# One layer of a diffusion backbone on one core: expert chunks of eight adjacent tiles, their inputs loaded a chunk ahead, and gate tables built in lagged steps

## The chip, the cores and the metric

The kernel runs on one core of one Trainium2 chip. The metric is device time in microseconds (us) from one execution; the engines are PE (matrix products, with weight loads shown as PEld), DVE (vector), ACT (scalar and activations), POOL and SP. SP, ACT and POOL also issue DMAs, each in its own program order, on queues that share 16 DMA engines.

## The reference, cut to what matters

The layer mixes tokens (attention and pooling, not touched here) and then runs a product-key expert sub-layer over 512 tokens. Each token has 8 heads with 16 experts each, out of 16,384; every expert is one row of `peer_u` and one row of `peer_v`:

```python
gate = jax.nn.softmax(top_s, axis=-1).astype(h.dtype)
u = peer_u[eidx]
act = jax.nn.gelu(jnp.einsum('thkd,td->thk', u, hb), approximate=False)
v = peer_v[eidx]
return jnp.einsum('thk,thkd->td', gate * act, v)
```

## The kernel before

The expert sub-layer takes two routes. For 160 of the tokens (called slots: 128 tokens, and 32 more packed four ways) POOL gathers the rows of `peer_u` and `peer_v` by indirect DMA, 1 MB each, and DVE multiplies them (L706) or accumulates them into `acc0` (L718). There are 320 such slots; `pump` deals them out between other work, each costing DVE one instruction over 2048 columns.

For the other 352 tokens (`TD`) the layer is computed densely. The 16,384 experts are 128 tiles of 128. A **U tile** (`u_tile`, L755) is 48 matmuls that give the activations of one tile for 352 tokens; ScalarE applies GELU (L757). The activations are multiplied by a dense table of gates (DVE, L959), split into a high and a low part (`split`: ACT L120 writes `a_hi`, DVE L121 writes `a_lo`), and a **V pass** (L976) multiplies them with `peer_v`. All products are made of three matmuls of high and low parts, so every weight block of 512 KB is loaded by SP into a `raw` buffer (L136), copied to `whi` by ACT (L120) and subtracted to `wlo` by DVE (L121). There are three `whi`/`wlo` pairs and, in the V stage, five raw buffers (three `raw`, one of `ub`, one `raw_v`).

Two stages matter. In the **spill stage** 72 U tiles are computed ahead, their activations written to `sg_s`, and between them `combine` builds the gate table: for four tokens at a time DVE compares index columns with a ramp (L, L804, one instruction for four tokens; R, L810, one per token, which also multiplies by the gate), PE forms `pg` from L and R (L811), ACT copies `pg` into `ge` (L812), and after 44 tokens `ge` (one buffer) goes to `g_s` by one DMA of 2,816 KB issued by ACT.

In the **V stage** the 128 tiles are taken in 16 chunks of eight (`CH`). A chunk is four fresh U tiles, then four tiles from `sg_s` (loaded by SP, L958, into three `sg` buffers that fresh tiles use too), then four passes `dq` over quarters of the output, each of 96 matmuls over the chunk's eight tiles; the last two chunks hold only kept tiles. The fresh tiles come first in a pass, the kept ones last. Sums go to `acc` by DVE (L987). After chunk 14 the gathered tokens are finished, after chunk 15 the dense ones.

A scheduler sets each engine's order from the program text; engines run their own list in order, so an instruction that waits holds everything behind it on its engine, the DMAs it issues included.

## Time and profile before

| | |
|---|---|
| runs (three) | 3627.98, 3633.67, 3633.84 us; median 3633.67 |
| profiled execution | 3620.55 us, of which the span from first to last instruction is 3618.8 |
| spill stage in the span | 1342 to 2048 us |
| V stage in the span | 2048 to 3602 us |
| mean granted PE clock | 0.977 of 2.4 GHz |

The span is one execution; a stage's length comes from the start of its first and last matmuls. A PE matmul of 352 columns is shown about 0.32 us long but the next one starts 0.16 us after it, since they overlap; so PE's pace is read from starts, or from counts in a stretch, and its losses from the idle time before an instruction and from the clock. A row of instructions reads: start, length, engine, line, operation, output and inputs; in square brackets stand the idle time before it and what ended it.

### The profile page before, as it was taken

To read this page: it belongs to the slowest core of one execution; us is meant where nothing else is said; L and a number is where in the kernel's file an instruction comes from. 1 tells how busy PE (TensorE), PEld (TensorE's weight loads), DVE (VectorE), ACT (ScalarE), POOL (GpSimd) and SP (SyncE) were. 2 spreads that over 40 slices of the span, in tenths; PEclk is the share of its full clock that TensorE was granted. 3 is DMA by queue.
4 is the path that set the end of the run, shared out by engine and by line. 5 is a ranking of instruction groups with operands and counts; after the bars stand their busy time and mean duration, and the time that the engine had idled before them with its cause. 6 is when DMAs were issued, how large, how long until landed. Compare 5 with 4: busy or idle time off the path is not lost.

```text
span 3618.8 us, 52598 instructions
## 1 busy us (share of the span) xinstructions
PE 3415.4 (94%) x20467; PEld 3159.7 (87%) x20467; DVE 2746.1 (76%) x4078; ACT 1383.3 (38%) x1981; POOL 562.5 (16%) x455
## 2 busy tenths in 40 slices
PE   7899999999998999999998999999999999999998
PEld 2588888899887889999988999899999998999998
DVE  5787787756536999997878677777777777877785
ACT  7455545455323234444443322233333222333343
POOL 1000000000031001211222222222212211222210
PEclk9999999999999999999999999999999999999999
DMA  9755555422547227889888879888878888888884
GB/s 338 266 174 171 177 169 179 149 66 75 197 140 252 83 91 260 299 321 345 322 312 309 323 289 336 305 305 296 312 296 315 304 308 313 323 309 307 313 309 166
DMA packets 267205, 916.01 MB, mean 253 GB/s; under 512 B 27666, under 2 KB 83707, under 8 KB 223179
## 3 DMA queue, kind: packets, MB, share of 16 engines
q1 hardware_dynamic: 157290, 469.45, 37.5%
q0 software_dynamic: 50208, 350.28, 25.5%
q10 hardware_dynamic: 59456, 92.92, 7.7%
q8 instruction: 160, 2.62, 0.3%
q14 instruction: 91, 0.74, 0.1%
HBM read 851.27 MB, written 49.71 MB: 249 GB/s over the span
## 4 chain that ended last, share of the span: by engine, by line
PE 57%; issue 15%; DMA 10%; DVE 10%; POOL 4%; ACT 3%; ACTq 0%; SPq 0%; POOLq 0%; DVEq 0%
PE pv L976 15%; PE pu L755 10%; PE pv L755 6%; PE zl L285 6%; PE pq L637 4%; PE zc L285 4%; PE pw L557 4%; DMA aw<-in_ada_dram 3%; DMA sg<-sg_s 2%; POOL row L700 2%; DMA g_s<-ge 2%; DVE wlo L121 2%; PE sc L373 2%; PE pg L811 1%; PE o L404 1%
## 5 line engine op out<-in xcount | busy, mean ns | idle before, releaser
L120 ACT CAST whi<-raw 128x1024 fp32r<-128x1024 f32 x591 | 619.2, 1050 | 1279.7 <-PE pv L976 467.9
L121 DVE TENSOR_TENSOR wlo<-raw,whi 128x1024 fp32r<-128x1024 f32 x591 | 732.3, 1245 | 333.7 <-ACT whi L120 331.9
L976 PE MATMUL pv<-a_hi,whi 128*128 128x352 f32 x2048 | 672.7, 331 | 35.9 <-ACT a_hi L120 30.2
L976 PE MATMUL pv<-a_lo,whi 128*128 128x352 f32 x2048 | 674.7, 330 | 31.3 <-DVE a_lo L121 31.2
L976 PE MATMUL pv<-a_hi,wlo 128*128 128x352 f32 x2048 | 668.6, 329 | 14.4 <-DVE wlo L121 14.3
L976 PEld LDWEIGHTS pv<-a_hi,whi 128*128 128x128 f32 x2048 | 392.9, 193 | 43.9 <-ACT a_hi L120 35.6
L976 PEld LDWEIGHTS pv<-a_lo,whi 128*128 128x128 f32 x2048 | 396.3, 194 | 38.3 <-DVE a_lo L121 38.3
L976 PEld LDWEIGHTS pv<-a_hi,wlo 128*128 128x128 f32 x2048 | 394.7, 193 | 19.6 <-DVE wlo L121 19.4
L755 PE MATMUL pu<-f_hi,whi 128*128 128x352 f32 x1152 | 380.7, 330 | 4.1 <-ACT whi L120 3.4
L755 PE MATMUL pu<-f_hi,wlo 128*128 128x352 f32 x1152 | 377.6, 328 | 6.9 <-DVE wlo L121 6.9
L755 PE MATMUL pu<-f_lo,whi 128*128 128x352 f32 x1152 | 375.8, 326 | 0.0
L718 DVE SCALAR_TENSOR_TENSOR acc<-row,w,acc 128x2048 f32<-128x2048 f32 x127 | 297.9, 2346 | 4.5 <-DMA row<-in_v_dram,eB 4.5
L755 PE MATMUL pv<-f_hi,wlo 128*128 128x352 f32 x896 | 290.4, 324 | 0.0
L755 PE MATMUL pv<-f_lo,whi 128*128 128x352 f32 x896 | 290.2, 324 | 0.0
L755 PE MATMUL pv<-f_hi,whi 128*128 128x352 f32 x896 | 289.1, 323 | 0.0
L706 DVE SCALAR_TENSOR_TENSOR row<-row,f 128x2048 f32<-128x2048 f32 x121 | 275.6, 2284 | 3.3 <-DMA row<-in_u_dram,e 3.3
L285 PE MATMUL zl<-h_hi,whi 128*128 128x512 f32 (+1 forms) x640 | 239.3, 374 | 0.0
L755 PEld LDWEIGHTS pu<-f_hi,wlo 128*128 128x128 f32 x1152 | 220.1, 191 | 9.4 <-DVE wlo L121 9.3
L755 PEld LDWEIGHTS pu<-f_hi,whi 128*128 128x128 f32 x1152 | 220.7, 192 | 6.0 <-ACT whi L120 5.0
L285 PE MATMUL zl<-h_lo,whi 128*128 128x512 f32 (+1 forms) x640 | 223.9, 350 | 0.0
L285 PE MATMUL zl<-h_hi,wlo 128*128 128x512 f32 (+1 forms) x640 | 223.8, 350 | 0.0
L755 PEld LDWEIGHTS pu<-f_lo,whi 128*128 128x128 f32 x1152 | 220.4, 191 | 0.0
(277 smaller groups left out, 6569.7 us busy)
## 6 DMA issues: line engine op xcount, KB each, us to landing
raw<-in_ut_dram SPq DMA_DIRECT2D x234, 512.0 KB
raw<-in_vd_dram SPq DMA_DIRECT2D x205, 512.0 KB
aw<-in_ada_dram SPq DMA_DIRECT2D x256, 256.0 KB
raw<-in_win_dram SPq DMA_DIRECT2D x80, 512.0 KB
aw<-in_ada_dram SPq DMA_DIRECT2D x64, 512.0 KB
raw_v<-in_vd_dram SPq DMA_DIRECT2D x51, 512.0 KB
g_s<-ge ACTq DMA_DIRECT2D x8, 2816.0 KB
gt<-g_s ACTq DMA_DIRECT2D x32, 704.0 KB
```

The costliest lines, as they stand in the source:

```text
L120: S.copy(dst_hi, src)
L121: V.tensor_sub(dst_lo, src, dst_hi.bitcast(F32))
L285: E.matmul(part[0], x[:, k8, :], y[:, k, part[1]], start=k == 0 and p == 0, stop=k == KT - 1 and p == 2)
L373: E.matmul(sc[:, cs], x[:, m, qs], y[:, cs], start=p == 0, stop=p == 1)
L404: E.matmul(po[:, b, :], aT[:, kb, b * 128:(b + 1) * 128], d["vn"][:, kb, :], start=kb == 0, stop=kb == 5)
L557: E.matmul(pw[b], x[:, k, bs], y[:, j, :], start=i + j == 0 and p == 0, stop=i + j == KT - 1 and p == 2)
L637: E.matmul(pq[:, cs], a[:, k8, :], b[:, k, cs], start=k == 0 and p == 0, stop=k == KT - 1 and p == 2)
L700: G.indirect_dma_start(out=row, out_offset=None, in_=table, in_offset=bass.IndirectOffsetOnAxis(ap=e[:, j:j + 1], axis=0))
L706: tc.keep_in_program_order(V.scalar_tensor_tensor(row, row, 1.0, f0, op0=OP.mult, op1=OP.mult, accum_out=s0[:, j:j + 1]))
L718: tc.keep_in_program_order(V.scalar_tensor_tensor(acc0, row, w0[:, j:j + 1], acc0, op0=OP.mult, op1=OP.add))
L755: E.matmul(pu, a[:, k8, :], b[:, k, :], start=k == 0 and p == 0, stop=k == KT - 1 and p == 2)
L976: E.matmul(pv[i], x[:, j, ks], y, start=n + j == 0 and p == 0, stop=n + j == CH - 1 and p == 2)
```

## The change

1. **Chunks.** A chunk is now eight adjacent tiles. `KEPT` says how many of each chunk are kept ones (6, 4, 4, 4, repeated): 72 in all as before, but spread over all 16 chunks, and they come first in the chunk. The fresh tiles (two or four) come last.
2. **Loads.** The gates of a chunk come by one DMA (one buffer `gt` for eight tiles), the kept activations in pairs into `sk` buffers of their own. ACT issues them, in the chunk before: the gates in pass 0, the pairs in passes 1 to 3. SP issues no activations any more.
3. **Gating** of kept tiles is done in pairs (128x704), between the U tiles; that of a fresh tile is put behind the next weight block (`owing`).
4. **`raw_v` is gone**: four raw buffers in the V stage, as in the spill stage.
5. **Combining.** R becomes one comparison of four tokens on DVE (L828), and ACT scales it by the gate, four instructions (L831). The products follow one step later and the copy to `ge` two steps after that, with four `pg` buffers for two. `ge` stays one buffer.
6. **The end.** The gathered slots finish in chunk 15, and so does `first_end` (the code that stood after chunk 14). `g2c` is made in the spill stage; `few_end_steps` (not shown) uses the `eq` buffers.

```diff
-SPILL = 72
 CH = 8
+KEPT = (6, 4, 4, 4) * 4
+SPILL = sum(KEPT)
...
-RATE = (SLOTS - (SPILL - PRE - GS) * GRATE) / (2 * NKEY - SPILL - 11)
+RATE = (SLOTS - (SPILL - PRE - GS) * GRATE) / (2 * NKEY - SPILL - 8)
+LAG = 2
...
-            sg = ub.tile([128, NG, TG], F32, name="sg", bufs=3)
+            return pu
+        def activated(pu):
+            sg = ub.tile([128, NG, TG], F32, name="sg", bufs=2)
             S.activation(sg.rearrange("p a t -> p (a t)"), pu, AF.Gelu)
             return sg
         def spill(n):
             for _ in range(n):
-                ib = next(run_ahead)
-                sg = u_tile(ib, psU.tile([128, TD], F32, name="pu", bufs=2))
-                nc.scalar.dma_start(sg_s[ib], sg.rearrange("p a t -> p (a t)"))
-        run_ahead = iter(range(SPILL))
+                i, ib = next(run_ahead)
+                sg = activated(u_tile(ib, psU.tile([128, TD], F32, name="pu", bufs=2)))
+                nc.scalar.dma_start(sg_s[i], sg.rearrange("p a t -> p (a t)"))
+        run_ahead = iter(list(enumerate(CH * c + i for c, k in enumerate(KEPT) for i in range(k))))
...
             def combine():
+                ready, made = [], []
+                def products():
+                    g, t4, L, R = ready.pop(0)
+                    pg = ps.tile([128, 4, 128], F32, name="pg", bufs=LAG + 2)
+                    for i in range(4):
+                        E.matmul(pg[:, i, :], L[:, i, :], R[:, i, :], start=True, stop=True)
+                    made.append((g, t4, pg))
+                def copied():
+                    g, t4, pg = made.pop(0)
+                    if t4 == 0:
+                        ges[g] = gb.tile([128, 128, TG], F32, name="ge", bufs=1)
+                    S.copy(ges[g][:, :, t4:t4 + 4].rearrange("p b t -> p t b"), pg)
+                    if t4 + 4 == TG:
+                        nc.scalar.dma_start(g_s[g], ges[g])
+                ges = {}
                 for g in range(NG):
-                    ge = gb.tile([128, 128, TG], F32, name="ge", bufs=1)
                     for t4 in range(0, TG, 4):
-                        m = min(4, TG - t4)
-                        pg = ps.tile([128, 4, 128], F32, name="pg", bufs=2)
-                        L = gb.tile([128, 4, 128], F32, name="L", bufs=2)
                         b, t = divmod(T - TD + g * TG + t4, 128)
-                        V.tensor_tensor(L, iota[:, None, :].to_broadcast([128, 4, 128]),
-                                        picks[b][:, 0, t:t + 4, None].to_broadcast([128, 4, 128]), op=OP.is_equal)
-                        for i in range(m):
-                            b, t = divmod(T - TD + g * TG + t4 + i, 128)
-                            pT = picks[b]
-                            R = gb.tile([128, 128], F32, name="R", bufs=6)
-                            V.tensor_scalar(R, iota, pT[:, 1, t:t + 1], pT[:, 2, t:t + 1], op0=OP.is_equal, op1=OP.mult)
-                            E.matmul(pg[:, i, :], L[:, i, :], R, start=True, stop=True)
-                        S.copy(ge[:, :, t4:t4 + m].rearrange("p b t -> p t b"), pg[:, 0:m, :])
-                        if t4 + 4 < TG:
-                            yield
-                    nc.scalar.dma_start(g_s[g], ge)
+                        pT = picks[b]
+                        L, R = (gb.tile([128, 4, 128], F32, name=n, bufs=3) for n in ("L", "R"))
+                        for x, i in ((L, 0), (R, 1)):
+                            V.tensor_tensor(x, iota[:, None, :].to_broadcast([128, 4, 128]),
+                                            pT[:, i, t:t + 4, None].to_broadcast([128, 4, 128]), op=OP.is_equal)
+                        for i in range(4):
+                            S.activation(R[:, i, :], R[:, i, :], AF.Copy, scale=pT[:, 2, t + i:t + i + 1])
+                        if ready:
+                            products()
+                        if len(made) > LAG:
+                            copied()
+                        ready.append((g, t4, L, R))
+                        yield
+                while ready or made:
+                    if ready:
+                        products()
+                    copied()
                     yield
...
-            nsteps = NG * ((TG + 3) // 4)
+            nsteps = NG * (TG // 4) + LAG + 1
...
-        more.append(lambda shape: fn.tile(shape, F32, name="raw_v"))
...
-            fresh, kept = list(range(SPILL, NKEY)), list(range(SPILL))
-            order = []
-            while fresh:
-                order += fresh[:4] + kept[:4]
-                fresh, kept = fresh[4:], kept[4:]
-            order += kept
             NC = NKEY // CH
+            first = [sum(KEPT[:c]) for c in range(NC)]
+            gts, sks = {}, {}
+            def load_gates(c):
+                if c < NC:
+                    gts[c] = ab.tile([128, NG, CH * TG], F32, name="gt", bufs=1)
+                    tc.keep_in_program_order(nc.scalar.dma_start(gts[c], g_s[:, :, c * CH:(c + 1) * CH, :].rearrange("a p b t -> p a (b t)")))
+            def load_kept(c, ps_):
+                for p in ps_ if c < NC else ():
+                    if 2 * p < KEPT[c]:
+                        sks[c, p] = ab.tile([128, 2, TD], F32, name="sk", bufs=max(KEPT) // 2)
+                        i = first[c] + 2 * p
+                        tc.keep_in_program_order(nc.scalar.dma_start(sks[c, p], sg_s[i:i + 2].rearrange("b p t -> p b t")))
+            def gated(c, n, m, sg, A):
+                V.tensor_tensor(sg.rearrange("p b (a t) -> p b a t", a=NG), sg.rearrange("p b (a t) -> p b a t", a=NG),
+                                gts[c][:, :, n * TG:(n + m) * TG].rearrange("p a (b t) -> p b a t", b=m), op=OP.mult)
+                hi, lo = A[n // 2]
+                split(hi[:, n % 2:n % 2 + m, :], lo[:, n % 2:n % 2 + m, :], sg)
+            def first_end():
...
+            load_gates(0)
+            load_kept(0, range(4))
             for c in range(NC):
-                ibs = order[c * CH:(c + 1) * CH]
+                ibs = list(range(c * CH, (c + 1) * CH))
                 last = c == NC - 1
-                A = []
-                for n, ib in enumerate(ibs):
-                    if n % 4 == 0:
-                        gt = ab.tile([128, NG, 4 * TG], F32, name="gt", bufs=2)
-                        nc.scalar.dma_start(gt, g_s[:, :, ib:ib + 4, :].rearrange("a p b t -> p a (b t)"))
-                    if ib >= SPILL:
-                        sg = u_tile(ib, bank()[:, 0:TD])
-                    else:
-                        sg = ub.tile([128, NG, TG], F32, name="sg", bufs=3)
-                        nc.sync.dma_start(sg.rearrange("p a t -> p (a t)"), sg_s[ib])
-                    V.tensor_mul(sg, sg, gt[:, :, (n % 4) * TG:(n % 4 + 1) * TG])
-                    a_hi = ab.tile([128, TD], F32R, name="a_hi", bufs=CH + 1)
-                    a_lo = ab.tile([128, TD], F32R, name="a_lo", bufs=CH + 1)
-                    split(a_hi, a_lo, sg.rearrange("p a t -> p (a t)"))
-                    A.append((a_hi, a_lo))
-                    if ib >= SPILL:
-                        pump(RATE)
+                A = [tuple(ab.tile([128, 2, TD], F32R, name=n, bufs=CH // 2) for n in ("a_hi", "a_lo")) for _ in range(CH // 2)]
+                owing = []
+                for j in range(CH - KEPT[c]):
+                    n = KEPT[c] + j
+                    pu = u_tile(ibs[n], bank()[:, 0:TD])
+                    pump(RATE)
+                    while owing:
+                        owing.pop(0)()
+                    for p in range(j, KEPT[c] // 2, CH - KEPT[c]):
+                        gated(c, 2 * p, 2, sks[c, p], A)
+                    owing.append(lambda n=n, pu=pu: gated(c, n, 1, activated(pu).rearrange("p a t -> p (a t)")[:, None, :], A))
+                while last and done[0] < SLOTS:
+                    pump(1)
                 for dq in range(4):
                     pp = [banks()[:, :, 0:TD] for _ in range(2)]
                     pv = [pp[i // 2][:, i % 2, :] for i in range(4)]
                     for n in range(0, CH, 2):
                         hi, lo = weights(vd[ibs[n] // 2, dq], [128, 2, 512])
                         for j in range(2):
-                            a_hi, a_lo = A[n + j]
+                            a_hi, a_lo = (x[:, j, :] for x in A[n // 2])
                             for i in range(4):
                                 ks = slice(i * 128, (i + 1) * 128)
                                 for p, (x, y) in enumerate(((hi, a_hi), (hi, a_lo), (lo, a_hi))):
                                     E.matmul(pv[i], x[:, j, ks], y, start=n + j == 0 and p == 0, stop=n + j == CH - 1 and p == 2)
-                        pump(0.5 * RATE)
+                        if not last:
+                            pump(0.5 * RATE)
+                        while owing:
+                            owing.pop(0)()
+                        if n == 4:
+                            if dq == 0:
+                                load_gates(c + 1)
+                            else:
+                                load_kept(c + 1, (dq - 1,))
                         if last and n == 2 and dq:
                             turned(dq - 1, fg)
                     if last:
+                        if dq == 0:
+                            first_end()
                         fg = final_g(dq)
...
-                if c == NC - 2:
-                    while done[0] < SLOTS:
-                        pump(1)
-                    for dq in range(4):
```

What moves is shown at three places. The first is SP's list in one V chunk. Before (`sg` are the kept activations, all else weight blocks):

```order
L136 DMA raw_v<-in_vd_dram 128x1024
L136 DMA raw<-in_vd_dram 128x1024 x3
L136 DMA raw_24646<-in_vd_dram 128x1024
L958 DMA sg<-sg_s 128x352 x2
L136 DMA raw_v<-in_vd_dram 128x1024
L136 DMA raw<-in_vd_dram 128x1024
L958 DMA sg<-sg_s 128x352 x2
L136 DMA raw<-in_vd_dram 128x1024 x2
L136 DMA raw_24806<-in_vd_dram 128x1024
```

and in the changed kernel:

```order
L138 DMA raw<-in_vd_dram 128x1024 x2
L138 DMA raw_23963<-in_vd_dram 128x1024
L138 DMA raw<-in_vd_dram 128x1024 x3
L138 DMA raw_24095<-in_vd_dram 128x1024
L138 DMA raw<-in_vd_dram 128x1024 x3
```

The activations have left SP's list, and with them `raw_v`. They stand on ACT's list now, in the passes of the chunk before (`gt` the gates, `sk` a pair of kept tiles, `sg` a fresh one):

```order
L122 CAST whi<-raw_20852 128x1024
L763 ACTIVATE sg<-pv 128x352
L122 CAST a_hi<-sg 128x352
L968 DMA gt<-g_s 128x8x352
L122 CAST whi<-raw 128x1024 x3
L122 CAST whi<-raw_20984 128x1024
L975 DMA sk<-sg_s 128x2x352
L122 CAST whi<-raw 128x1024 x3
L122 CAST whi<-raw_21116 128x1024
L975 DMA sk<-sg_s 128x2x352
L122 CAST whi<-raw 128x1024 x3
L122 CAST whi<-raw_21246 128x1024
```

The second place is DVE's list in one V chunk. Before, at the turn from the last fresh tiles to pass 0 (`row` and `acc` are gather slots):

```order
L959 TENSOR_TENSOR sg<-sg,gt 128x352 x3
L121 TENSOR_TENSOR wlo<-raw_v,whi 128x1024
L121 TENSOR_TENSOR a_lo<-sg,a_hi 128x352
L706 SCALAR_TENSOR_TENSOR row_12694,s_13314<-row_12694,f_9445 128x2048
L121 TENSOR_TENSOR a_lo<-sg,a_hi 128x352 x2
L121 TENSOR_TENSOR wlo<-raw,whi 128x1024
L959 TENSOR_TENSOR sg<-sg,gt 128x352
L706 SCALAR_TENSOR_TENSOR row_12693,s_13314<-row_12693,f_9445 128x2048
L121 TENSOR_TENSOR a_lo<-sg,a_hi 128x352
L959 TENSOR_TENSOR sg<-sg,gt 128x352
L121 TENSOR_TENSOR wlo<-raw,whi 128x1024
L121 TENSOR_TENSOR a_lo<-sg,a_hi 128x352
```

and in the changed kernel, in passes 1 and 2 of the chunk before:

```order
L979 TENSOR_TENSOR sk<-sk,gt 128x704
L123 TENSOR_TENSOR wlo<-raw,whi 128x1024
L709 SCALAR_TENSOR_TENSOR row_12694,s_13305<-row_12694,f_9445 128x2048
L1045 TENSOR_TENSOR accT<-accT,pv 128x704 x2
L123 TENSOR_TENSOR wlo<-raw_21926,whi 128x1024
L709 SCALAR_TENSOR_TENSOR row_12695,s_13305<-row_12695,f_9445 128x2048
L123 TENSOR_TENSOR wlo<-raw,whi 128x1024
L979 TENSOR_TENSOR sk<-sk,gt 128x704
L123 TENSOR_TENSOR wlo<-raw,whi 128x1024
L709 SCALAR_TENSOR_TENSOR acc_12692,s_13305<-acc_12692,f_9445 128x2048
L123 TENSOR_TENSOR wlo<-raw,whi 128x1024
L1045 TENSOR_TENSOR accT<-accT,pv 128x704 x2
```

Four multiplications of kept tiles stood within pass 0 ahead of weight blocks; now each pair is multiplied one chunk earlier. The third place is one stretch of combining. DVE before:

```order
L804 TENSOR_TENSOR L<-iota,pT 128x512
L810 TENSOR_SCALAR R<-iota,pT 128x128 x4
L121 TENSOR_TENSOR wlo<-raw,whi 128x1024
L804 TENSOR_TENSOR L<-iota,pT 128x512
L810 TENSOR_SCALAR R<-iota,pT 128x128 x2
L121 TENSOR_TENSOR wlo<-raw,whi 128x1024
L718 SCALAR_TENSOR_TENSOR acc_12691<-row_12693,w_13313,acc_12691 128x2048
L810 TENSOR_SCALAR R<-iota,pT 128x128 x2
L804 TENSOR_TENSOR L<-iota,pT 128x512
```

The same on DVE in the changed kernel:

```order
L123 TENSOR_TENSOR wlo<-raw,whi 128x1024
L828 TENSOR_TENSOR R<-iota,pT 128x512
L123 TENSOR_TENSOR wlo<-raw,whi 128x1024
L828 TENSOR_TENSOR L<-iota,pT 128x512
L828 TENSOR_TENSOR R<-iota,pT 128x512
L123 TENSOR_TENSOR wlo<-raw,whi 128x1024
L721 SCALAR_TENSOR_TENSOR acc_12692<-row_12694,w_13304,acc_12692 128x2048
L123 TENSOR_TENSOR wlo<-raw_15959,whi 128x1024
L828 TENSOR_TENSOR L<-iota,pT 128x512
L828 TENSOR_TENSOR R<-iota,pT 128x512
```

Four R instructions have become one. Their multiplication by the gate stands on ACT (four L831 for one step, between the copies of weights):

```order
L831 ACTIVATE R<-R,pT 128x128 x4
L122 CAST whi<-raw 128x1024
L763 ACTIVATE sg<-pu 128x352
L817 COPY ge<-pg 128x4x128
L770 DMA sg_s<-sg 128x352
L831 ACTIVATE R<-R,pT 128x128 x4
L122 CAST whi<-raw 128x1024
L122 CAST whi<-raw_15225 128x1024
```

The copies to `ge` follow a tile's GELU there, and each belongs to a step made earlier.

## Rows read from the trace of the kernel before

**Rows 1.** The page's first lines: busy time of each engine over the whole span.
```profile
span 3618.8 us, 52598 instructions
PE 3415.4 (94%) x20467; PEld 3159.7 (87%) x20467; DVE 2746.1 (76%) x4078; ACT 1383.3 (38%) x1981; POOL 562.5 (16%) x455
```

**Rows 2.** Busy time by stretch, for the spill stage and the V stage: length, busy time and count of PE, PEld, DVE, ACT, POOL, then granted PE clock, DMA engines' busy share, GB/s.
```profile
1342.00:2048.00 706.00, 661.03 (x4189) 649.05 (x4187) 603.28 (x918) 284.38 (x332) 144.20 (x99) 0.97 0.84 308
2048.00:3602.00 1554.00, 1472.44 (x8867) 1451.66 (x8868) 1183.04 (x1114) 480.08 (x593) 316.04 (x223) 0.97 0.82 302
```

**Rows 3.** What PE's matmuls waited for in the V stage: us in total, times, longest.
```profile
PE pv L976 <- DVE a_lo L121: 31.2, 20, 4.2
PE pv L976 <- ACT a_hi L120: 30.2, 16, 5.9
PE pv L976 <- DVE wlo L121: 14.3, 10, 3.1
PE pv L976 <- ACT whi L120: 5.6, 9, 1.0
```

**Rows 4.** Busy time by stretch, columns as in rows 2: chunks 1, 13 and 15.
```profile
2153.30:2255.40 102.10, 95.72 (x578) 94.55 (x577) 77.59 (x81) 30.40 (x36) 22.71 (x16) 0.97 0.84 308
...
3373.70:3471.20 97.50, 94.02 (x578) 92.20 (x577) 80.83 (x73) 32.66 (x41) 24.52 (x16) 1.00 0.89 334
...
3536.40:3602.10 65.70, 65.70 (x421) 65.18 (x420) 40.01 (x55) 24.55 (x40) 0.00 (x0) 1.00 0.43 141
```

**Rows 5.** The same columns: the four U tiles of chunk 1, then the four V passes of chunks 1, 10 and 13.
```profile
2153.40:2184.10 30.70, 30.70 (x193) 30.70 (x193) 22.09 (x24) 10.96 (x14) 7.04 (x4) 1.00 0.63 236
...
2184.10:2255.40 71.30, 64.92 (x386) 63.75 (x385) 55.41 (x57) 19.44 (x22) 15.67 (x13) 0.95 0.93 340
...
3104.60:3172.70 68.10, 64.33 (x385) 63.14 (x385) 56.03 (x45) 19.47 (x22) 14.39 (x13) 0.97 0.96 357
3404.50:3471.20 66.70, 63.22 (x385) 61.40 (x385) 58.49 (x53) 21.70 (x27) 17.31 (x13) 1.00 1.00 379
```

**Rows 6.** DVE in order of time, in pass 0 of chunk 4.
```profile
2507.24 0.53 DVE L959 TENSOR_TENSOR sg<-sg,gt 128x352 f32<-128x352 f32 x1 [3.39 <-DMA sg<-sg_s]
2507.68 1.39 DVE L121 TENSOR_TENSOR a_lo<-sg,a_hi 128x352 fp32r<-128x352 f32 x3
...
2513.52 0.52 DVE L959 TENSOR_TENSOR sg<-sg,gt 128x352 f32<-128x352 f32 x1 [2.25 <-DMA sg<-sg_s]
```

**Rows 7.** SP's DMA issues at the same place (the length of a row of two reaches from the first issue to the end of the second).
```profile
2498.18 0.33 SPq L136 DMA_DIRECT2D raw<-in_vd_dram  x1
2498.61 9.94 SPq L958 DMA_DIRECT2D sg<-sg_s  x2
2515.21 0.33 SPq L136 DMA_DIRECT2D raw<-in_vd_dram  x1
```

**Rows 8.** PE in order of time, at the same place.
```profile
2508.25 0.66 PE L976 MATMUL pv<-a_lo,whi 128*128 128x352 f32 x1 [3.52 <-DVE a_lo L121]
...
2509.30 0.49 PE L976 MATMUL pv<-a_lo,whi 128*128 128x352 f32 x1
2509.59 0.49 PE L976 MATMUL pv<-a_hi,wlo 128*128 128x352 f32 x1
...
2511.91 0.32 PE L976 MATMUL pv<-a_hi,whi 128*128 128x352 f32 x1
2512.07 0.32 PE L976 MATMUL pv<-a_lo,whi 128*128 128x352 f32 x1
```

**Rows 9.** What PE's matmuls waited for in the spill stage, columns as in rows 3.
```profile
PE pg L811 <- ACT ge L812: 13.4, 5, 7.2
PE pg L811 <- DVE R L810: 11.4, 7, 4.3
PE pu L755 <- DVE wlo L121: 6.9, 8, 3.8
PE pt L835 <- DVE zB L836: 4.6, 1, 4.6
PE pv L921 <- ACT sg L757: 4.5, 1, 4.5
PE pu L755 <- ACT whi L120: 3.4, 2, 2.7
```

**Rows 10.** Groups of instructions in the spill stage, DVE's and then ACT's: count, busy time and mean ns of one, idle time before them and what ended it.
```profile
L810 DVE TENSOR_SCALAR R<-iota,pT 128x128 f32<-128x128 f32 x352 | 103.6, 346 | 18.0 <-PE pg L811 17.9
...
L804 DVE TENSOR_TENSOR L<-iota,pT 128x512 f32<-128x512 f32 x88 | 59.8, 679 | 0.0
...
L120 ACT CAST whi<-raw 128x1024 fp32r<-128x1024 f32 x145 | 151.0, 1049 | 286.9 <-PE pu L755 242.5 <-DMA g_s<-ge 8.4 <-issue 6.7
L812 ACT COPY ge<-pg 128x512 f32<-128x512 f32 x88 | 97.2, 1145 | 75.0 <-DMA g_s<-ge 53.3 <-PE pg L811 13.0 <-PE pu L755 8.6
...
L682 ACT ACTIVATE gt<-gt 128x128 f32<-128x128 f32 x3 | 0.9, 309 | 5.8 <-DVE gt L681 5.8
```

**Rows 11.** ACT in order of time at the turn from the spill stage to the V stage.
```profile
2029.31 0.33 ACTq L815 DMA_DIRECT2D g_s<-ge  x1
...
2044.83 0.38 ACTq L953 DMA_DIRECT2D gt<-g_s  x1
2045.30 1.04 ACT L120 CAST whi<-raw 128x1024 fp32r<-128x1024 f32 x1 [8.36 <-DMA g_s<-ge]
```

More of the change, by code (lines that the diff above doesn't have):

```diff
@@ L658, in body @@
         gateB = gp.tile([128, GB], F32, name="gateB")
+        g2c = gp.tile([128, KT], F32, name="g2c")
         eB = gp.tile([128, GB], I32, name="eB")
@@ L823, in few_end_steps @@
                     V.tensor_add(sel, sel, ident[:, q * GB:(q + 1) * GB])
-                z = gb.tile([128, D], F32, name="zB")[0:GB, :]
+                zs = [rt.tile([128, 4, 16, 16], F32, name="eq", bufs=2).rearrange("p h k i -> p (h k i)")[0:GB, :] for _ in range(2)]
                 ss = gb.tile([128, 4], F32, name="ssB")[0:GB, :]
@@ new lines, in first_end @@
+            def first_end():
+                for dq in range(4):
+                    ds = slice(dq * 512, (dq + 1) * 512)
+                    V.tensor_mul(acc0[:, ds], acc0[:, ds], by_column("fg", m_s[:, 3 * D + dq * 512:3 * D + (dq + 1) * 512]))
+                    V.tensor_add(acc0[:, ds], acc0[:, ds], residual(0, 128, dq))
+                    jk = fn.tile([128, 512], F32, name="tm", bufs=2)
+                    S.activation(jk, acc0[:, ds], AF.Square, accum_out=fss[3][:, dq:dq + 1])
+                rs = final_rstd(3, 128)
+                for dq in range(4):
+                    scaled_out(acc0, 0, 128, dq, rs, final_g(dq))
```

33 lines of the change are left out of this document (12 added, 21 removed).

## The prediction

> **What bounds the kernel now.** I read the page's busy shares first: PE is busy for 94% of the span, DVE for 76% and ACT for 38% [rows 1]. A PE that is so busy leaves room only in what it waits for and in its clock, so I went to the stretches by stage. The change lies in two of them, the spill stage (706 us) and the V stage (1554 us); both run at a mean granted clock of 0.97, with DMA shares of 0.84 and 0.82 [rows 2].
>
> PE's own pace is read where nothing disturbs it. Four U tiles are 192 matmuls and take 30.7 us at full clock with PE busy throughout [rows 5], 0.160 us each; the starts at full clock stand 0.16 us apart too [rows 8]. A chunk's four V passes are 384 matmuls, so 61.4 us; they take 66.7 to 71.3 us [rows 5]. So U tiles lose nothing and V passes 5 to 10 us a chunk. Chunk 15 has all its inputs early and takes 65.7 us with 36 small transposes, PE busy throughout [rows 4]. For the stage: 56 U tiles and 16 times four passes are 8832 matmuls, 1413 us, and 4 us for those transposes. Of 1554 us, 137 are lost.
>
> The list of PE's waits says to whom: 31.2 us on `a_lo`, 30.2 on `a_hi`, 14.3 on `wlo`, 5.6 on `whi` [rows 3], 81.3 in all. The clock adds (1 - 0.97) x 1554 = 47 us, which makes 128 of the 137. One place shows the mechanism. DVE stands still for 3.39 us until a kept tile lands, and for 2.25 us for the next [rows 6]; what it then writes is what PE waits 3.52 us for [rows 8]. SP is caught as well: it holds its list from 2498.61 to 2508.55, because a kept tile's load waits for one of three `sg` buffers, and the next weight load leaves only at 2515.21 [rows 7]. After PE's wait the starts stand 0.29 us apart, not 0.16 [rows 8]: the lower clock level, 1.2 GHz. So a wait costs more than its idle time, 128/81.3 = 1.57 times.
>
> By the Trainium skill (TensorE: Matmul & The Clock Gate, Part 1: The HAM clock gate) half the clock is what an idle array falls to, and activity gives the rest back. The trace agrees with that; if it did not, only the idle 61 us would stand in the first term below.
>
> **The change part by part.** *Kept tiles a chunk early, own buffers, first in the chunk.* The waits on `a_hi` and `a_lo` are 61.4 of 81.3 us, a share of 0.755. In the changed order a kept pair is multiplied in passes of the chunk before, and only the last fresh tile's chain (GELU, gate, two splits) remains; it is needed at the last weight block, behind three blocks of 24 matmuls, 11.5 us. I take all of these waits off: 0.755 x 128 = 97 us. Bounds: 61 (idle time alone) and 103 (the same share of 137).
>
> *The waits on `wlo` and `whi` stay:* 19.9 x 1.57 = 31 us, 2.0 a chunk, though SP is no longer held. Whether they shrink is a rival below.
>
> *Bytes in the V passes.* 340 GB/s over 71.3 us are 24.2 MB, at a DMA share of 0.93 [rows 5]. Passes of 61.4 + 2.0 us would need 382 GB/s; the highest row has 379, at a share of 1.00. U stretches have room (236 GB/s, 0.63), but only what four raw buffers hold can be moved there. I add 1 us a chunk, 14 us; bounds 0 and the second rival.
>
> *One raw buffer less:* 0. The spill stage runs on the same four, and there ACT's copies wait for PE (242.5 us), not for a weight load [rows 10].
>
> *Gates of the first chunk.* Their load can't be early: it follows the spill stage directly, and DVE's first kept multiplication waits for it with U-tile weights queued behind. How long 1,408 KB take the trace doesn't show. A kept tile of 176 KB, issued at about 2508.2, is used at 2513.52, 5 us [rows 6, 7]; 2,816 KB took 15.5 us from 2029.31 to 2044.83 [rows 11]. I take the middle, 10.5 us, of which PE bridges about 7.7 with two weight blocks, and add the clock and the pairs that follow: 8 us, bounds 0 and 15.
>
> *Combining.* Idle time in the spill stage adds up to 44.2 us [rows 9] and the clock to 0.03 x 706 = 21, so here a wait costs 1.47 times its idle time. The waits on R, 11.4 us, go, since products follow a step later: 17 us. DVE also sheds 88 x (4 x 346 - 679) ns = 62 us of its 603 [rows 2, 10], hidden behind PE. The wait at the turn to the V stage, 4.5 us, came from the first gate load on ACT, which waited for the last `g_s` write with weight copies queued behind it, 8.36 us [rows 9, 11]; four more U tiles now stand between the two: 7 us. The waits on `ge`, 13.4 us, come from the one `ge` buffer: ACT stands still for the write, 53.3 us in six waits [rows 10]. That stays, and weight copies still stand behind it; but with four `pg` buffers PE can use up its weights first. Of 13.4 x 1.47 = 20 I take 5, bounds 0 and 20. Together 29, bounds 0 and 44.
>
> *Scaling on ACT* is 352 x 0.309 = 109 us, by the nearest activation of 128x128 [rows 10], on an engine busy for 284 of 706 us: 0. The cover is the lead of weight copies over PE. Were it gone, a step would put four scalings, 1.24 us, in front of a copy, 109 us in all; the lower bound of 0 above contains part of that.
>
> *Fewer, wider gate and split instructions* and the end moved into chunk 15 (12 DVE instructions, 8 us at the price of L804; DVE is busy for 40 of 65.7 us there [rows 4]): 0.
>
> Sum: -97 - 29 + 14 + 8 = -104 us. Against the profiled execution, 3620.55 us, that is 3516.5; that execution is 13 us below the median of the runs, so the difference is taken from the median: 3633.67 - 104 = 3530 us.
>
> **The rivals.** *The DMA engines bind the V passes (0.22).* For it: shares of 0.93 and 0.96 in two of three rows. Then PE waits for weights in place of `a_lo`, and passes settle at 68.1 us as in chunk 10, not 64.4. They average (1554 - 430)/16 = 70.2 now, so 16 x 2.1 = 34 us are won, with the others -55: 3579 us. Against it: chunk 13 ran at 379 GB/s, 66.7 us, with only 3.5 us not busy [rows 5].
>
> The Trainium skill (DMA: Bandwidth & Descriptors, Issuing engines are not separate DMA queues) speaks for this rival: whoever issues them, DMAs share 16 engines, and another issuer saves only sequencer time. The row of 1.00 agrees that there is nothing beyond; rows 7 show what the sequencer's hold costs.
>
> *More goes than I count (0.13).* With SP never held, the `wlo` waits vanish too and bytes spread over the U stretches: 31 + 14 us more, 3485 us.
>
> *The waits come back under another name (0.04):* DVE waits for `sk` where it waited for `sg`. Only the spill gain is left: 3633.67 - 29 + 8 = 3613 us.
>
> *The gate load is late (0.05), slower.* All eight tiles' gates come at once into a single buffer. From issue to use there are about five weight blocks of 3.84 us, 19 us, and PE goes on for two more, 7.7. By eight times the kept tile's 5 us it would land after 40: PE loses 13 x 1.57 = 21 us in each of 15 chunks, and the kernel is some 200 us slower. It decides at 31 us, where 4.4 x 1.57 x 15 eats the 104. Against it: twice the bytes took 15.5 us [rows 11].
>
> **How the numbers follow.** The forecast has 0.56, with 3505 to 3560 of its own from its bounds. The range reaches to the DMA rival and to the richer case: 3487 to 3588. About 0.2% (7 us) is what a measurement can tell from no change. Faster 0.93 (the first four cases, less a rest), same 0.02, slower 0.05.
>
> **What would show it.** Right: PE's waits on `a_hi` and `a_lo` under 10 us, on R under 4; V passes of a middle chunk at 63 to 66 us, U stretches at 30.7; SP issuing weights alone, with no hold of 10 us; idle time before `ge` still about 50 us; one wait at the first chunk's gates. Wrong: waits on `wlo` or `whi` that grow to 60 us or more with DMA at a share of 1.00 in the passes (the first rival), DVE idle before the kept multiplication ended by `gt` in every chunk (the last), or ACT's copies late behind L831 in the spill stage.

## The result, and the profile after

The changed kernel takes 3507.49 us (median of 4 runs, 3502.01 to 3510.15), the kernel before 3633.76: a ratio of 0.965, with a 95% interval of 0.963 to 0.967. The forecast was 3530, with a range of 3487 to 3588. The profiled execution is 3508.51 us, at its median, while that of before lay 13 us under its own. So the medians differ by 126 us, the two traces by 112; readings below are of the traces. (Runs of before alone spread from 3617 to 3639 in the later comparisons.)

The page's first lines, to be held against [rows 1]:

```profile
span 3506.7 us, 52462 instructions
PE 3368.6 (96%) x20467; PEld 3132.0 (89%) x20467; DVE 2695.9 (77%) x3742; ACT 1476.9 (42%) x2295; POOL 576.9 (16%) x455
```

Busy time of the spill stage and the V stage, columns as in [rows 2]:

```profile
1342.00:2027.60 685.60, 653.76 (x4199) 643.73 (x4197) 572.45 (x667) 386.61 (x682) 170.62 (x100) 0.99 0.85 316
2027.60:3490.00 1462.40, 1432.20 (x8869) 1428.20 (x8870) 1166.23 (x1039) 471.30 (x557) 303.55 (x223) 0.99 0.87 321
```

The spill stage gave 20 us, the V stage 92. (Both spill rows begin at 1342 us. Its first matmul stands at 1342.2 before and at 1344.6 after; from there the stage takes 683 us for 706.) PE's waits in the V stage [rows 3]:

```profile
PE pv L1024 <- DVE wlo L123: 22.2, 8, 4.4
PE pv L758 <- DVE wlo L123: 6.8, 1, 6.8
PE pv L758 <- ACT sg L763: 1.3, 1, 1.3
PE pv L1024 <- DVE a_lo L123: 0.8, 1, 0.8
```

`a_hi` and `a_lo` went from 61.4 us to 0.8. Chunks 0, 1, 3 and 13 (chunk 0 has two U tiles, 480 matmuls; the others four, 576) [rows 4], then the U tiles and the passes of chunk 3 [rows 5]:

```profile
2027.70:2119.90 92.20, 81.50 (x479) 80.34 (x480) 64.66 (x64) 24.26 (x27) 17.37 (x13) 0.94 0.87 329
2120.10:2216.90 96.80, 93.64 (x576) 93.36 (x575) 74.81 (x75) 29.90 (x34) 18.16 (x15) 0.98 0.85 318
2309.10:2401.00 91.90, 91.90 (x577) 91.90 (x576) 78.53 (x79) 30.58 (x35) 20.04 (x16) 1.00 0.91 339
3202.20:3301.10 98.90, 94.68 (x577) 94.39 (x576) 75.62 (x60) 29.80 (x34) 20.19 (x15) 0.97 0.83 310
...
2309.10:2339.80 30.70, 30.70 (x194) 30.70 (x193) 27.64 (x30) 11.54 (x15) 7.16 (x6) 1.00 0.85 309
2339.80:2401.10 61.30, 61.30 (x386) 61.30 (x385) 50.99 (x50) 19.05 (x20) 12.88 (x10) 1.00 0.94 354
```

Chunk 3 loses nothing: 576 matmuls at 0.160 us. Eight chunks, with this one, are like it (76.5 us where there are two U tiles), and so is chunk 15 but for its transposes. Chunk 0 loses 15 us, and six others (1, 5, 6, 9, 12, 13) 1.4 to 7.4 each, 31 together. One such place, in chunk 12: DVE, ACT's issues of the gates and of the pair, and PE, each in order of time; the DMA share of the six us from 3149; and what three DMA queues moved from 3144 to 3156 (packets, MB, share of the 16 engines; q0 the gathers of POOL, q1 SP's weights, q10 ACT's loads):

```profile
3154.80 1.22 DVE L123 TENSOR_TENSOR wlo<-raw,whi 128x1024 fp32r<-128x1024 f32 x1
3167.38 0.89 DVE L979 TENSOR_TENSOR sk<-sk,gt 128x704 f32<-128x704 f32 x1 [11.36 <-DMA sk<-sg_s]
3168.18 1.22 DVE L123 TENSOR_TENSOR wlo<-raw,whi 128x1024 fp32r<-128x1024 f32 x1
...
3137.99 0.37 ACTq L968 DMA_DIRECT2D gt<-g_s  x1
...
3149.30 0.37 ACTq L975 DMA_DIRECT2D sk<-sg_s  x1
...
3169.46 0.66 PE L1024 MATMUL pv<-a_hi,wlo 128*128 128x352 f32 x1 [4.39 <-DVE wlo L123]
3169.92 0.49 PE L1024 MATMUL pv<-a_hi,whi 128*128 128x352 f32 x1
3170.21 0.49 PE L1024 MATMUL pv<-a_lo,whi 128*128 128x352 f32 x1
...
3149.00:3155.00 6.00, 6.00 (x39) 6.00 (x38) 5.93 (x6) 2.11 (x2) 0.00 (x0) 1.00 1.02 407
...
q0 software_dynamic: 390, 2.93, 59.8%
q1 hardware_dynamic: 395, 1.44, 29.9%
q10 hardware_dynamic: 401, 0.56, 12.6%
```

A pair issued at 3149.30 lands only at about 3167.3, 18 us later, with the DMA engines full. DVE comes to its multiplication at 3156.02, 6.7 us behind the issue, so DVE stands still for 11.36 us and the weight split behind it is late by 4.39 for PE. After that PE starts 0.29 us apart again, the lower clock level.

The row of the wait names the pair, but the gates are the larger part of the cause. DVE's multiplication needs both, and by the trace's landings the gates, issued at 3137.99, are there only at 3166.40, 28 us later and 1 us ahead of the pair, which stands behind them on ACT's queue. Without the pair DVE would, by these times, have stood for 10.4 us all the same. In all five chunks with such a wait (1, 5, 9, 12, 13) the gates take 24 to 28 us and land 0.7 to 1.0 us ahead of the pair; in the other chunks from 2 to 14 they take 18 to 21. What differs is the gathers of POOL: they move 4.6 to 5.2 MB while the gates of the five are under way, and 2.6 to 3.4 MB in the others. That the gathers make the gates late is the likely reading; no run here changes the gathers alone.

DVE's wait for a chunk's first pair and PE's idle time go together: 9.4 to 11.4 us on DVE are 2.9 to 4.4 on PE (in the five chunks), 7.3 are 2.1 (in chunk 0), 5.0 and less are nothing. The splits that are finished ahead of PE cover 5 to 7 us there. (The first wait of all, 15.1 us at the start of chunk 0, is 6.8 on PE.) Chunk 6 is another case: its 1.0 us on PE stand behind 5.29 us in which DVE waits for a gather. In total for the V stage, DVE's waits after the change, and then before it:

```profile
DVE sk L979 <- DMA sk<-sg_s: 110.3, 20, 15.1
```

```profile
DVE sg L959 <- DMA sg<-sg_s: 69.1, 26, 7.1
```

In the spill stage, PE's waits [rows 9] and two groups of ACT [rows 10]:

```profile
PE pu L758 <- ACT whi L122: 13.7, 5, 5.9
PE pu L758 <- DVE wlo L123: 12.6, 9, 3.8
PE pt L861 <- DVE eq L862: 2.3, 1, 2.3
PE pv L758 <- ACT sg L763: 1.3, 1, 1.3
PE pu L758 <- ACT sg L763: 1.0, 1, 1.0
PE pg L810 <- ACT R L831: 0.9, 2, 0.6
...
L831 ACT ACTIVATE R<-R,pT 128x128 f32<-128x128 f32 x352 | 113.2, 391 | 49.8 <-DVE R L828 45.4 <-issue 1.9 <-ACT sg L763 0.4
L817 ACT COPY ge<-pg 128x512 f32<-128x512 f32 x88 | 97.2, 1152 | 29.0 <-DMA g_s<-ge 24.5 <-DVE L L828 3.2 <-PE pg L810 0.8
```

R has nearly gone from the list (11.4 to 0.9). `ge` is gone by name, but `whi` and `wlo` grew from 10.3 to 26.3 us.

### The profile page after: what moved, and what is told of

It is laid out like the page before. It is cut to its first block, busy times and chain, and to the rows that moved or that the text cites. A ratio compares the mean times of both kernels' runs of the same rounds, so it can differ in the third digit from the quotient of the medians.

```text
span 3506.7 us, 52462 instructions
## 1 busy us (share of the span) xinstructions
PE 3368.6 (96%) x20467; PEld 3132.0 (89%) x20467; DVE 2695.9 (77%) x3742; ACT 1476.9 (42%) x2295; POOL 576.9 (16%) x455
## 5 line engine op out<-in xcount | busy, mean ns | idle before, releaser
L122 ACT CAST whi<-raw 128x1024 fp32r<-128x1024 f32 x664 | 696.0, 1050 | 1342.1 <-PE pv L1024 623.9
L123 DVE TENSOR_TENSOR wlo<-raw,whi 128x1024 fp32r<-128x1024 f32 x664 | 821.7, 1242 | 290.2 <-ACT whi L122 288.8
L1024 PE MATMUL pv<-a_lo,whi 128*128 128x352 f32 x2048 | 663.6, 324 | 0.8 <-DVE a_lo L123 0.8
L1024 PE MATMUL pv<-a_hi,whi 128*128 128x352 f32 x2048 | 664.2, 324 | 0.0
L758 PE MATMUL pu<-f_hi,whi 128*128 128x352 f32 x1152 | 378.9, 329 | 14.7 <-ACT whi L122 13.7
L1024 PEld LDWEIGHTS pv<-a_lo,whi 128*128 128x128 f32 x2048 | 388.3, 190 | 1.1 <-DVE a_lo L123 1.1
```

Of the source, the lines that this page charges most:

```text
L122: S.copy(dst_hi, src)
L123: V.tensor_sub(dst_lo, src, dst_hi.bitcast(F32))
L758: E.matmul(pu, a[:, k8, :], b[:, k, :], start=k == 0 and p == 0, stop=k == KT - 1 and p == 2)
L1024: E.matmul(pv[i], x[:, j, ks], y, start=n + j == 0 and p == 0, stop=n + j == CH - 1 and p == 2)
```

## The experiments

Each was timed beside the kernel before on the same chip, whose medians were 3628.43 (e1 to e4), 3628.19 (e5 to e8) and 3628.71 (e9 to e11).

**e1: the combining alone.** The kernel before with `combine()` of the changed kernel, its `nsteps` and `LAG`, and its `few_end_steps` (for room).

> The kernel before with the new combining alone (steps that lag, R compared for four tokens at once and scaled on ACT, four pg buffers, the later end's buffers); chunks and loads of the V stage are those of before. Theory: the two halves of the change are independent. The spill stage shortens from 706 us to about 686 as in the changed kernel, the V stage stays at 1554, and the time is 3634 - 20 = 3614 us (3606 to 3622). PE's waits on R vanish, those on ge turn into waits on whi and wlo, since ACT still stands still for the g_s write. Rival: ACT's 352 scalings only pay off because the V stage's turn changed too; then the spill stage stays within 5 us of 706 and the time at 3629 to 3640.

Measured 3614.78 us, ratio 0.996 (0.994 to 0.998). From its first matmul the spill stage takes 687 us; in this trace it begins 5 us later, so the V stage starts 13.7 us earlier than before. R's wait is 0.7 us and `whi` and `wlo` have 27.8. The theory held for the spill stage; the V stage, which this edit leaves alone, took 1561 us in the trace for 1554.

**e2: the V stage alone.** The changed kernel with `combine()` and `nsteps` of before.

> The changed kernel with the old combining (R on DVE with its gate, product in the same step, two pg buffers); chunks, loads and gating of the V stage are the changed ones. Theory: the V stage takes its 1462 us as in the changed kernel, the spill stage its 706, so 3634 - 92 = 3542 us (3532 to 3550). Rival: DVE, which carries 62 us more in the spill stage, is late at the turn, and the turn's gate load finds the last g_s write unfinished; then the first chunk grows from 92 us by 5 or more and the time is 3550 to 3565.

Measured 3527.92, ratio 0.972 (0.969 to 0.974): 14 us under the expected time by the medians, and 4 under its range. Its trace has a spill stage of 705 us and a V stage of 1464, as expected, and its span is 91 us under that of before. The rest is spread: the median of before was 3628 here, not 3634, its profiled execution lies 8 us under that, and e2's own lies 2 us above its median. The halves nearly add up: 13.7 and 100.5 by medians, or 114, against 121 to 126 for both.

**e3: the kept multiplication held in place.**

```
-                V.tensor_tensor(sg.rearrange(... gts[c] ...), op=OP.mult)
+                mul = V.tensor_tensor(sg.rearrange(... gts[c] ...), op=OP.mult)
+                if m == 2:
+                    tc.keep_in_program_order(mul)
```

> The changed kernel with one edit: a kept pair's multiplication by the gates is held on DVE behind what the program writes before it, so it stands between the U tiles of its own chunk, a chunk later than the scheduler put it. Theory: what is left in chunks 1 to 14 of the changed kernel (31 us of lost PE time, all after waits on wlo) is the old mechanism in a new place: DVE stands still for a pair that has not landed (110.3 us in 20 waits on sk) with weight splits queued behind it. Then every chunk from 1 on runs without a wait, at 91.9 us with four U tiles and 76.5 with two, DVE's waits on sk are under 20 us in all, and the time is 3507 - 31 = 3476 us (3468 to 3485). Rival: the wlo waits come from the DMA engines (share 0.93 in the passes), and DVE's stand is only where they show; then PE waits as long on wlo or whi and the time is 3500 to 3515. Second rival: multiplications in the U stretch delay the splits of U weights there: waits on wlo in the U tiles, time 3490 to 3520.

Measured 3476.55, ratio 0.958 (0.955 to 0.961). All of PE's waits from chunk 1 on, and the V stage:

```profile
PE pv L954 <- DVE row L955: 0.5, 1, 0.5
...
2030.70:3459.70 1429.00, 1420.41 (x8868) 1418.87 (x8868) 1167.72 (x1039) 474.06 (x556) 292.51 (x223) 1.00 0.89 328
```

Chunks 1 to 14 all take 91.9 or 76.5 us, and DVE waits for a pair once, 15.2 us in the first chunk. More bytes per us than before the edit (328 GB/s for 321) and no wait: the DMA engines did not bind PE through the weights. They made gates and pairs late, and DVE's list handed that on. Chunk 6, whose wait was on a gather, is clean too.

**e4: loads in their own chunk.** `load_gates(c)` and `load_kept(c, ...)` stand at the head of chunk c, and the ones in passes 0 to 3 are taken out.

> The changed kernel with the gates and kept pairs loaded at the start of their own chunk, not in the chunk before; buffers, pairs, the issuing engine and the order of the gating in the program stay. Theory: loading early is what took the a_hi and a_lo waits away. Without it every chunk has what the first chunk of the changed kernel has (a wait of 6.8 us on wlo in the second U tile, behind DVE's wait for sk; 13.6 us lost in all above the others): with half to all of that in 15 chunks the time is 3507 + 100 to 200 = 3610 to 3710 us. Rival: own buffers and the place behind the U tiles are enough, since a chunk of four U tiles has 30.7 us to cover a load that takes about 16; then 3500 to 3525 us.

Measured 3614.11, ratio 0.996 (0.995 to 0.998). All of the V stage's gain is lost: it takes 1564 us in the trace, 10 more than before, and the 14 us under the kernel before are those of the spill stage. ACT's issue of the two pairs of chunk 2 (the gates went just ahead, at 2209.38), DVE and PE there, and the total of PE's waits on it:

```profile
2209.78 4.71 ACTq L975 DMA_DIRECT2D sk<-sg_s  x2
...
2224.92 0.89 DVE L979 TENSOR_TENSOR sk<-sk,gt 128x704 f32<-128x704 f32 x1 [11.02 <-DMA sk<-sg_s]
...
2227.00 0.66 PE L758 MATMUL pv<-f_hi,wlo 128*128 128x352 f32 x1 [5.69 <-DVE wlo L123]
...
PE pv L758 <- DVE wlo L123: 99.9, 16, 7.2
```

DVE comes to its multiplication at 2213.90, 4.5 us behind the issue of the gates. Every chunk has such a wait, of 5.4 to 7.2 us on PE.

**e5: loads as in e4, gating behind the last U tile.** e4 and e3 together, with

```
-                    for p in range(j, KEPT[c] // 2, CH - KEPT[c]):
+                    for p in range(KEPT[c] // 2) if j == CH - KEPT[c] - 1 else ():
```

> As e4, gates and kept pairs loaded at the start of their own chunk, but all pairs are multiplied behind the last U tile of the chunk, held there on DVE. Theory: what costs e4 its 107 us is not that the loads come late but that DVE's list meets a pair before it has landed, 6 us after the chunk begins; a chunk of four U tiles has 30.7 us, more than the 15 that DVE waits there. Then the 12 chunks with four U tiles run at 91.9 us as in e3, the four with two U tiles (15.3 us) lose a few us each, and the time is 3477 + 10 to 35 = 3487 to 3512 us, far from e4's 3614. Rival: the loads' bytes, 2.1 MB packed into the U stretch, delay the weights themselves; then PE waits on whi and wlo in the U tiles of every chunk and the time stays above 3560.

Measured 3482.86, ratio 0.959 (0.958 to 0.961). That is 4 us under the expected range. A chunk of two U tiles takes 77.0 us, so even that lost nothing to speak of; the expected few us were wrong. Only the last chunk is clearly longer than in e3, 103 us for 97. Loads of chunk 1, on ACT, and its first multiplication:

```profile
2106.69 0.37 ACTq L968 DMA_DIRECT2D gt<-g_s  x1
2107.09 1.71 ACTq L975 DMA_DIRECT2D sk<-sg_s  x2
...
2146.03 0.88 DVE L979 TENSOR_TENSOR sk<-sk,gt 128x704 f32<-128x704 f32 x1
```

39 us lie between issue and use. With e4 this decides: what counts is the distance between the issue and its use on the engines' lists, not the chunk in which the load is written. 131 us separate e4 and e5, and the loads are in the same place.

**e6: SP issues the loads.** e3 with `nc.sync.dma_start` for `gt` and `sk`.

> As e3 (a chunk early, multiplications held in place), but SP issues the gates and the kept pairs, between its weight loads, in place of ACT. Theory: with own buffers the issuing queue matters little; SP is held for the one gate buffer once a chunk, some 5 to 10 us, less than the four raw buffers give (four blocks of 3.84 us), so chunks stay at 91.9 us and the time within 10 us of e3: 3470 to 3490. Rival: SP's hold was what cost PE its waits in the kernel before; then each chunk again loses 3 to 6 us on wlo or whi and the time is 3520 to 3570.

Measured 3475.19, ratio 0.957 (0.956 to 0.959), as e3. SP stood for the gate buffer for 0.8 us in all, not for 5 to 10 a chunk, so this run does not say what a longer hold of SP would cost. The Trainium skill (DMA: Bandwidth & Descriptors, Issuing engines are not separate DMA queues) says that transfers share the DMA engines whoever issues them, and that another issuer saves only sequencer time; this pair of runs agrees.

**e7: own buffers alone.** The kernel before with

```
-        more.append(lambda shape: fn.tile(shape, F32, name="raw_v"))
...
-                        sg = ub.tile([128, NG, TG], F32, name="sg", bufs=3)
+                        sg = ab.tile([128, NG, TG], F32, name="sk", bufs=4)
                         nc.sync.dma_start(sg.rearrange("p a t -> p (a t)"), sg_s[ib])
```

and two `sg` buffers for the fresh tiles.

> The kernel before with two edits: kept tiles are loaded by SP into four buffers of their own (two sg buffers are left for fresh tiles), and raw_v is gone to make the room; chunks, the old combining and the single-tile gating stay, and nothing holds an instruction in place. With own buffers the scheduler itself puts the loads of the next chunk into passes 0 and 1. Theory: that is most of the V stage's gain; the a_hi and a_lo waits go, DVE's waits for kept tiles remain (over 50 us) and show as waits on wlo, so the V stage takes 1465 to 1515 us instead of 1554 and the time is 3540 to 3590. Rival: adjacent tiles, pairs and the later place of a fresh tile's chain are what took the waits away; then the V stage stays above 1535 and the time is 3610 to 3640.

Measured 3548.48, ratio 0.978 (0.976 to 0.980). SP issues four kept tiles in a row, and DVE multiplies them 21 us later without a wait; PE's waits in the V stage:

```profile
2484.19 1.77 SPq L957 DMA_DIRECT2D sk<-sg_s  x4
...
2505.75 1.83 DVE L958 TENSOR_TENSOR sk<-sk,gt 128x352 f32<-128x352 f32 x4
...
PE pv L975 <- DVE wlo L121: 15.8, 14, 4.1
PE pv L975 <- ACT whi L120: 7.0, 4, 3.3
PE pv L975 <- DVE a_lo L121: 6.7, 5, 2.0
PE pv L920 <- ACT sg L757: 4.8, 1, 4.8
PE pv L975 <- ACT a_hi L120: 1.7, 2, 0.9
```

The V stage is 1478 us, so own buffers (with one raw buffer less) are worth 76 of its 92. I had expected DVE's waits for kept tiles to remain above 50 us; they are 6, and one of 11 for the gates.

**e8: e3, and a step more for the write.**

```
-                        if len(made) > LAG:
+                        while len(made) > (LAG + 1 if g and t4 == 12 else LAG):
                             copied()
...
-                    pg = ps.tile([128, 4, 128], F32, name="pg", bufs=LAG + 2)
+                    pg = ps.tile([128, 4, 128], F32, name="pg", bufs=LAG + 3)
```

> As e3, with one more edit in the spill stage: where a group of tokens ends, the first copy into the one ge buffer waits one step more (five pg buffers for four), so the g_s write has two steps, about 15 us, to finish before ACT asks for the buffer. Theory: ACT's stand for that write (24.5 us in six waits) and the weight copies queued behind it are what PE's waits on whi and wlo in the spill stage come from (13.7 and 12.6 us); with it gone ACT's idle time before ge is under 8 us, the spill stage shortens from 685 by 10 to 25 us, and the time is 3477 - 18 = 3459 us (3451 to 3467). Rival: those waits come from ACT's scalings and the two copies now made in one step, which put 3.5 us in front of a weight copy; then the spill stage stays at 680 to 690 and the time at 3472 to 3482.

Measured 3459.09, ratio 0.953 (0.952 to 0.955). ACT's copies to `ge`, and PE's wait:

```profile
L817 ACT COPY ge<-pg 128x512 f32<-128x512 f32 x88 | 96.5, 1164 | 16.3 <-DMA g_s<-ge 11.0 <-PE pu L758 3.8 <-ACT sg L763 1.0
...
PE pu L758 <- ACT whi L122: 3.1, 2, 2.1
```

ACT's idle time before `ge` is 16.3 us, 11.0 of it for the write (24.3 in e3), where I expected under 8 in all. It was enough: `whi` fell from 12.8 (e3) to 3.1, and the spill stage, from its first matmul, from 685 us to 667. `wlo` stayed at 10.7 (11.5 in e3), so those waits have another cause: ahead of the longer ones DVE is busy without a gap, the longest behind the picking of the experts, the others behind L828, the comparisons for L and R.

**e9: e8, and four U tiles in the first chunk.**

```
-KEPT = (6, 4, 4, 4) * 4
+KEPT = (4, 6, 4, 4) * 4
...
-                    for p in range(j, KEPT[c] // 2, CH - KEPT[c]):
+                    for p in range(j, KEPT[c] // 2, CH - KEPT[c]) if c else range(j - 2, j - 1) if j >= 2 else ():
```

> As e8, with one more edit: the first chunk has four kept and four fresh tiles, the second six and two (4, 6, 4, 4 in place of 6, 4, 4, 4 in the first four chunks, and so on), and the first chunk's two pairs are multiplied behind its third and fourth U tile. Theory: the first chunk's loss in e8 (11 us: a wait of 6.0 on wlo while DVE stands 15 us for the first pair) needs only cover; with four U tiles in front the pair has landed when DVE comes to it, so the first chunk runs at 92 to 95 us, the second at 76.5, and the time is 3459 - 10 = 3449 us (3444 to 3456). Rival: the wait comes from the DMA engines, which at the turn carry gates, pairs and weights for several passes at once; then PE waits there as long on whi or wlo and the time is 3456 to 3465.

Measured 3455.39, ratio 0.951 (0.949 to 0.954); the interval overlaps that of e8. The trace shows the step: the first chunk takes 94.2 us at a DMA share of 0.97, and the V stage is 1418 us (1427 in e8), where its 8832 matmuls and the transposes need 1417. The spill stage took 4 us more than in e8's trace, so the gain in time is not clear of the noise.

```profile
2019.00:2113.20 94.20, 92.62 (x576) 92.04 (x577) 72.31 (x71) 28.67 (x34) 18.90 (x15) 1.00 0.97 373
2019.00:3437.00 1418.00, 1416.42 (x8869) 1415.23 (x8870) 1166.14 (x1039) 474.36 (x557) 298.30 (x223) 1.00 0.89 331
```

This version beats both kernels: 52 us under the changed one.

**e10: R on DVE.** The changed kernel with four `V.tensor_scalar(R[:, i, :], iota, ..., op0=OP.is_equal, op1=OP.mult)` per step as before, in place of R's comparison and of L831.

> The changed kernel with R compared and multiplied by the gate on DVE, four instructions per step as before, no scalings on ACT; the steps still lag. Theory: the lag alone took the waits on R away, and the shift of work from DVE to ACT was worth nothing, since both have room; PE's waits on R stay under 2 us, the ones on whi and wlo behind the g_s write stay at 20 to 30 us, the spill stage at 678 to 690, the time at 3502 to 3514 us. Rival: DVE with 62 us more (86% busy) is late for weight splits; waits on wlo grow by 8 us or more and the time is 3518 to 3535.

Measured 3506.70, ratio 0.966 (0.964 to 0.968), the changed kernel's time. PE's wait on R is 3.3 us, a little over what I expected. The waits on `whi` and `wlo` are 19.7 us, at the lower end of the expected. ACT, with less to do, stands longer for the write (46.1 us for 24.5). Moving the scaling gained and cost nothing that this comparison can tell; the lag took most of R's waits away.

**e11: no lag of the copy.** `LAG = 0`, so two `pg` buffers.

> The changed kernel with the copy to ge following its product in the same step and two pg buffers in place of four; the product still comes a step after its R. Theory: four pg buffers only moved the wait for the g_s write, from PE's products to its weights; with two, PE waits on ge through pg again, 8 to 15 us, and less on whi and wlo, so the spill stage changes by less than 6 us and the time is 3502 to 3514 us. Rival: the lag did part of the work; then PE's waits add up to more, the spill stage is 690 to 700 and the time 3516 to 3526.

Measured 3516.64, ratio 0.968 (0.966 to 0.971), with an interval that overlaps the changed kernel's. The time lies at the edge of the rival's range, the spill stage in the theory's. The wait did come back under its old name, and `whi` and `wlo` shrank to 11.2:

```profile
PE pg L810 <- ACT ge L817: 15.3, 6, 5.3
```

PE's waits in the stage add up to 28 us, for 31 in the changed kernel. The spill stage is 5 us longer in the trace, and so is the V stage, which the edit leaves alone. Whether the lag is worth those first 5 us or nothing stays open.

## Why the prediction was right, and where it was off

**The main term held.** The `a_hi` and `a_lo` waits went, 61.4 to 0.8 us, and DVE's held list was what made them. SP's hold, which the prediction named beside it, mattered little by itself: in e7 SP still stands 73 us ahead of its loads of kept tiles (94 before), DVE's waits for these tiles fall from 69.1 to 6.3, and `a_hi` and `a_lo` fall to 8.4 us.

**"A kept pair is multiplied in passes of the chunk before" was taken for a gain; it was the flaw.** DVE's waits for kept tiles grew from 69.1 to 110.3 us. My third rival, that DVE waits for `sk` where it waited for `sg`, was at work in five chunks, and the fourth, gates that land late, with it: its 19 us from issue to use are 18.0 in chunk 12, and the gates took 28. Together they cost 30 of the 31 us that e3 won back in chunks 1 to 14. The cost stayed small because the gates took 24 to 28 us there and not 40, and because the wait now meets DVE with weight splits ahead of PE. The 31 us that I let stand for `wlo` and `whi` came out at 31, but by chance: I took them for waits that the change leaves alone, and e3 shows them to be the flaw of the change.

**The time of a load.** I took 5 us for a kept tile and 10.5 for the gates. [Rows 6] and [rows 7] hold a second tile, issued at 2498.61 and used as it landed at 2507.24, 8.6 us, that I passed over. The first chunk's gates took 14.6 us by the landings, later ones 18 to 28, and a pair 18 in a pass with full DMA engines. That term failed in kind: a load's time is that of the stretch it falls into and of what stands ahead of it on its queue. The first chunk lost 15 us; with 2.0 for weights I had 10.

**The bytes, +14, cost nothing.** Clean passes take 61.3 us, less than the 63 to 66 that I gave, at 354 GB/s and a share of 0.94. I had written that only what four raw buffers hold can move to the U stretches. There, 236 GB/s over 30.7 us became 309: 7.2 MB became 9.5, and the passes fell from 24.2 to 21.7 MB. What moved, in the two chunks compared (1 before, 3 after), was not weights, 4.07 MB and 4.15 in the U stretch, but gathers of POOL, 3.14 and 5.30, which my sum left out. So the first rival (DMA engines bind) was out, and the second, richer one was half right: the bytes spread, the `wlo` waits stayed.

So of the 137 us lost in the V stage I left 62, and 45 are left: bytes -14, first chunk +5, the others about +1, and 9 that I could not place and that are gone.

**Spill: 29 forecast, 20 measured** (23 from the stage's first matmul). PE's idle time there fell from 44.9 us (44.2 in [rows 9], and 0.7) to 31.8; 13.1 times the 1.47 of the forecast are 19. R gave 10.5 us of idle time (10.5 x 1.47 = 15, forecast 17), the turn 3.2 (5, forecast 7). The 5 us that I credited to four `pg` buffers were wrong: 13.4 us on `ge` went, and `whi` and `wlo` took 16.0 more. e8 shows that the larger part of them came from the write (24.3 in e3, 13.8 in e8), and that 17 us could be had. "0" for ACT's scalings is confirmed by e10 (113 us measured, 109 estimated); one sign was wrong, the idle time before `ge`, which I saw at about 50 us and which is 29.0, 24.5 of it for the write, since the copy now stands behind the scalings in ACT's list (55.5 without them, in e10). Confirmed is also "0" for one raw buffer less, by the chunks without a loss.

**The sum.** -104 was forecast in trace terms, and the traces show -112. That is nearer than its parts, by luck: the V stage gave 92 us where I had 75, the spill stage 20 where I had 29. The other 14 us of the median's 126 are the spread of executions of before: I subtracted from the median, which is right only if both profiled executions lie alike to their medians.

## What to carry to other kernels

When a load is made earlier, look at where the instruction that uses it stands on its engine's list: an early use brings the wait forward, and everything behind it on that list pays, whatever buffer it needs. Hold the use back until the load has surely landed, counting its time from the busiest stretch it can fall into and from the loads ahead of it on its queue. When one buffer is written out and refilled, a wait that is moved from one engine to another is not removed; give the write time by delaying the refill.

## What the runs showed of the hardware

Issuing a load took ACT 0.37 us in the passes, but 8.55 us for three of them at the turn to the V stage, where gates, pairs and weights were asked for at once. The issues in the changed kernel, and the weight copy behind them:

```profile
2028.51 8.55 ACTq L975 DMA_DIRECT2D sk<-sg_s  x3
...
2037.15 1.05 ACT L122 CAST whi<-raw 128x1024 fp32r<-128x1024 f32 x1 [9.52 <-issue]
```

In e4, where the pairs follow the gates at once in every chunk, two issues took 4.71 us in the place shown; in e5, for chunk 1, 1.71. So an issue is not always short for the engine that makes it. Why it was long there, the runs don't show.

The three queues of chunk 12 moved nearly the same number of packets from 3144 to 3156, 390, 395 and 401, but 2.93, 1.44 and 0.56 MB: the packets of the gathers are up to 8 KB, those of the weights 4 KB, those of gates and pairs 1.4 KB. So ACT's loads got 47 of 412 GB/s there. A load in small packets was slow beside loads in large ones; whether larger packets would make it faster, no run here shows.
